# Hybrid encoder trunk on one core: M4 parts of four late pairs kept in freed operand slots, row block 0 of the last block finished first, one page's place in the plan, and one wide attention product

## The chip, the core and the metric

The kernel runs on one NeuronCore of a Trainium2 chip. The metric is device time in microseconds (us). The kernel before has a median of 2621.29 us over three runs (2619.23 to 2624.82).

The engines, as the profile names them: PE multiplies matrices (PEld loads its stationary operand beside it), DVE is the vector engine, ACT the scalar engine, POOL the general one; SP only issues DMAs, POOL issues some too. Each engine takes its instructions strictly in the order in which the program wrote them. An instruction whose input is not there holds everything behind it on that engine.

## What is computed

Two layers over `x` (256 rows of 4096). In each layer one wide input projection, then two kinds of heads, then an output projection added to the input; a last norm at the end.

```python
for l in range(DEPTH):                        # DEPTH = 2
    h = rmsnorm(x, norm_w[l])
    proj = h @ w_in[l]                        # 4096 x 11264
    aq, ak, av, ag, rq, rk, rv, rg = jnp.split(proj, SPLIT_POINTS, axis=-1)
    ...                                       # axial rope, qk-norm
    a_out = silu(ag) * gqa_attention(aq, ak, av)
    r_out = silu(rg) * rmsnorm(bidirectional_retention(rq, rk, rv), ret_norm[l])
    x = x + jnp.concatenate([a_out, r_out], axis=-1) @ w_out[l]   # 4096 x 4096
return rmsnorm(x, final_norm)
```

## The kernel before, in words

**Blocks, pairs and pages.** A projection is cut into blocks of 1024 output columns: 11 for each input projection and 4 for each output projection, 30 in all. The four projections are phases 0 to 3. Within a block the 4096-long contraction is cut into 16 pairs of 256. For a pair, rows (two blocks of 128), contraction (two halves) and columns (two of 512) are the 2x2x2 blocks of a matrix product. A "seven" pair (7 or 8 of the 16) forms it with seven block products M1 to M7 in Strassen's manner; the other, "eight" pairs use eight products that go into the banks M2 to M5. M1 to M7 are seven PSUM banks, which add up over all 16 pairs. A weight page is 128x1024 f32: an eight pair has the pages A and B, a seven pair A, T, B and U, of which T and U are sums (`wsum`) that DVE makes from the two loaded pages.

**Split numbers.** Every f32 operand is split in two fp32r numbers: the high part (`whi`, `fhi`, `whb`) is a cast on ACT, the low part (`wlo`, `wlb`) is source minus high part on DVE. "Far" pages take a road without DVE: ACT casts (`fhi`), ACT writes minus that (`flo`), and a DMA on POOL's queue adds the source to it. The activations are split in the same way and kept in SBUF all phase long (`x7h`/`x7l` for sevens, `x8h`/`x8l` for eights, `xm` for one mixed pair). A product is three matmuls of 128x512: high x high, high x low, low x high.

**The end of a block.** `combining` adds the banks into two result tiles, in the order M1 (copied by ACT), M6, M7, and then M3, M5 (two adds), M4, M2. In PE's stream the last pair (15) is sorted by that same bank order, so that its pages A and B alternate: M3 of A, M3 of B, M5 of A, and so on. The next block starts with M1 and M3 of pair 0, and then needs M3, M5, M4, M2 for page A of pair 1: a bank may be started again only once its add is done.

**What sets the order.** The program plans while it is written: every engine has a clock with a cost per instruction, and each time an engine's clock is the earliest, `pick` chooses what it does next. Weight operations have a key, the planned time of their page (`g.at`) less a lead. Everything else runs in lanes, generators that yield the engine they want next; `Lane.step` works out from when on a lane may go on. `urgent` lanes, `combining` among them, go before weight operations. So a change of a planned time moves instructions in all of the program.

**The last block** (phase 3, block 3) has its own end, `last_combining`. For the last four eight pairs (7, 9, 11, 13) the products into M4 are left out at first and done at the very end from four extra pages, PAGE_E, which are loaded and split a second time. Banks are finished in the order M2, M5, M3, M4, so that the upper 128 rows (row block 0) are complete before M4 is. `finish(m)` then squares, sums, takes the power -0.5 on POOL, scales eight tiles of 128x512 and stores them, all by DMAs on SP's queue.

**Attention values.** `attention_values` multiplies the transposed probabilities with the values, for two heads e, with a product of 256 columns for each.

Of the kernel before, what the change touches and what calls it, by code (L numbers as in the profile page):

```python
# [12 lines left out]
F32R = mybir.dt.float32r  # L13
# [169 lines left out]

def pages_in_order(phase, first=False, last=False):
    late = [_p for _p in range(NP - 1) if _p not in SEVENS[phase]][-LATE_PAIRS:] if last else []
# [7 lines left out]
    for _p, _k in order:  # L193
        if _p in SEVENS[phase] and _p not in skip:
            yield _p, _k, [(_b, (ALL, _a), _h) for _b, _a, _pg, _h in SEVEN_PRODUCTS if _pg == _k]
        else:
# [3 lines left out]
                if _pg == _k and not (_p in late and _b == "M4")  # L200
            ]
    for _p in late:
        yield _p, PAGE_E, [("M4", (_i, 1), _i) for _i in range(2)]
# [3 lines left out]
FINAL_ORDER = ("M2", "M5", "M3", "M4")  # L207
# [115 lines left out]
def hybrid_encoder(  # L323
# [184 lines left out]
    class Weights:  # L508


        def __init__(self):
            self.pages, at = [], 0.0
            for phase in range(2 * DEPTH):
                w = w_out if phase % 2 else w_in
                for b in range(N_OUT2 if phase % 2 else N_IN):
                    start = (phase, b) == (0, 0)
                    end = (phase, b) == (2 * DEPTH - 1, N_OUT2 - 1)
                    for n, (p, k, uses) in enumerate(pages_in_order(phase, start, end)):
# [7 lines left out]
                        at += (MM4 if g.direct else 3 * MM[NB]) * len(uses)  # L526
                        self.pages.append(g)
            self.raws, self.highs, self.sums, self.fars = Slots(RAWS), Slots(HIGHS), Slots(SUMS), Slots(FAR)
            self.lows, self.halves = Slots(LOWS), Slots(HALVES)
            self.todo, self.ops = [], {"V": [], "A": [], "F": []}  # L530
# [35 lines left out]
        def load(self, most=99):  # L566
            while self.todo and most and self.raws.ready():
# [5 lines left out]
                if g.kind == PAGE_E:  # L573
                    step = 1
                for i in range(0, 2, step):
                    n = i if g.kind == PAGE_E else k
                    at = dma("sync", r[:, i : i + step, :], g.src[n, :, i : i + step, :])
# [41 lines left out]
        def high_ready(self, g):  # L619
            s = self.source(g)[0]  # L620
            return s is not None and s[1]() and (self.halves if self.half(g) else self.highs).ready()

        def high(self, g):
# [5 lines left out]
            else:  # L629
                self.highs.take()  # L630
                g.hi = t(wp, [P, 2, NB], "whi", HIGHS, F32R)
            ac.copy(g.hi, f32(src))
# [7 lines left out]
        def low(self, g):  # L640
# [4 lines left out]
            else:  # L645
                self.lows.take()
                g.lo = t(wp, [P, 2, NB], "wlo", LOWS, F32R)
            ve.tensor_sub(g.lo, src, f32(g.hi))
# [10 lines left out]
        def far_ready(self, g):  # L659
            return self.has(g, "raw") and self.fars.ready()  # L660

        def far_parts(self, g):
            self.fars.take()
            src = f32(g.raw[0])
            g.hi = t(wp, [P, 2, NB], "fhi", FAR, F32R)
            g.lo = t(wp, [P, 2, NB], "flo", FAR, F32R)
            ac.copy(g.hi, src)
# [4 lines left out]
        def far_low(self, g):  # L672
            ac.activation(g.lo, f32(g.hi), AF.Copy, scale=-1.0)
            self.adds.append((ac.done, g))

        def add(self):
            while self.adds and self.adds[0][0] <= now.t:
                g = self.adds.pop(0)[1]
                g.low_at = dma("gpsimd", g.lo, g.src[1], accum_op=ALU.add)
# [30 lines left out]
    class Lane:  # L710
# [4 lines left out]
        def __init__(self, steps, need=0, own=0, owner=None, after=0.0, hurry=False, due=1e9, start=lambda: True):  # L715
            self.hurry, self.start, self.due = hurry, start, due
            self.steps, self.need, self.own, self.owner = steps, need, own, owner
            self.begun, self.done, self.want, self.at, self.last = False, False, 0.0, after, after

# [13 lines left out]
        def step(self):  # L733
# [515 lines left out]
    def attention_values(g, h, kv, sgT):  # L1249
# [8 lines left out]
        for e in range(2):  # L1258
            for k in range(MT):
                product(  # L1260
                    o[:, e, :].rearrange("p (k t) -> p k t", t=BLK),
                    at(v, ALL, k),
                    [in_both(w, 2 * e + k) for w in parts],
                    k == 0,
                    k == MT - 1,
                )
# [249 lines left out]
    def block(after_pair, phase, first_order=False, order=LAST_ORDER, last=None):  # L1516
# [9 lines left out]
        for p, k, uses in pages_in_order(phase, first_order, last is not None):  # L1526
            if k == PAGE_E:
                rest_units += [(p, k, use, "H") for use in uses] + [(p, k, use, "L") for use in uses]
                continue
# [16 lines left out]
        for p, k, _, _ in units:  # L1546
            left[p] = left.get(p, 0) + 1
            uses[p, k] = uses.get((p, k), 0) + 1
# [388 lines left out]
```

## Time and profile before

| | us |
|---|---|
| median of three runs | 2621.29 |
| the profiled execution | 2623.02 |
| its span in the profile | 2621.2 |
| PE busy | 2582.6 |
| DVE busy | 2323.9 |
| ACT busy | 1910.0 |
| POOL busy | 436.2 |

The table's busy times can be read against the span: PE has work in nearly all of it, and DVE in nearly nine tenths. A matmul's end is modelled, so that a busy PE need not be one at full rate. Two things are to be kept apart when PE is read: time in which it waits, and time in which its granted clock is below one.

### The profile page before, as it was taken

To read this page: it belongs to the slowest core of one execution; us is meant where nothing else is said; L and a number is where in the kernel's file an instruction comes from. 1 tells how busy PE (TensorE), PEld (TensorE's weight loads), DVE (VectorE), ACT (ScalarE), POOL (GpSimd) and SP (SyncE) were. 2 spreads that over 40 slices of the span, in tenths; PEclk is the share of its full clock that TensorE was granted. 3 is DMA by queue.
4 is the path that set the end of the run, shared out by engine and by line. 5 is a ranking of instruction groups with operands and counts; after the bars stand their busy time and mean duration, and the time that the engine had idled before them with its cause. 6 is when DMAs were issued, how large, how long until landed. Compare 5 with 4: busy or idle time off the path is not lost.

```text
span 2621.2 us, 34650 instructions
## 1 busy us (share of the span) xinstructions
PE 2582.6 (99%) x11570; PEld 2124.0 (81%) x11570; DVE 2323.9 (89%) x2908; ACT 1910.0 (73%) x2672; POOL 436.2 (17%) x592
## 2 busy tenths in 40 slices
PE   9999999999999999999999999999999999999997
PEld 5788888888888888788788888888888888877886
DVE  7898988998888889888998889989989888997888
ACT  8777776777767688666877776767768676886665
POOL 0112211221211110221111211212212121101110
PEclk9999999999999999999999999999999999999999
DMA  9999999998898898999999999989989988989997
GB/s 298 309 296 284 273 285 281 272 300 265 279 281 267 282 272 247 296 281 279 309 270 281 287 277 290 276 267 299 282 263 283 279 263 281 283 243 273 268 275 237
DMA packets 214227, 729.62 MB, mean 278 GB/s; under 512 B 25760, under 2 KB 32544, under 8 KB 214048
## 3 DMA queue, kind: packets, MB, share of 16 engines
q1 hardware_dynamic: 149200, 523.44, 56.7%
q0 software_dynamic: 64848, 203.98, 34.3%
q8 instruction: 90, 1.47, 0.2%
q14 instruction: 89, 0.73, 0.1%
HBM read 679.08 MB, written 48.23 MB: 277 GB/s over the span
## 4 chain that ended last, share of the span: by engine, by line
PE 80%; DVE 7%; issue 4%; DMA 4%; ACT 2%; POOL 1%; SPq 0%; DVEq 0%; ACTq 0%; POOLq 0%
PE M L1111 77%; DVE wlo L232 3%; PE ps L1111 3%; DMA wraw<-in_w_in 1%; DVE wsum L232 1%; DMA pT<-p_dram 1%; ACT whi L232 1%; DMA flo<-in_w_in 1%; DVE cb L232 1%; DMA q<-q_dram 0%; DVE ca L232 0%; ACT fhi L232 0%; DMA q_dram<-cb 0%; DVE x8l L232 0%; DVE wlb L232 0%
## 5 line engine op out<-in xcount | busy, mean ns | idle before, releaser
L232 ACT CAST whi<-wraw 128x1024 fp32r<-128x1024 f32 x525 | 547.0, 1048 | 203.8 <-PE M L1111 172.8
L232 DVE TENSOR_TENSOR wlo<-wraw,whi 128x1024 fp32r<-128x1024 f32 x525 | 636.2, 1220 | 51.7 <-ACT whi L232 24.9
L232 DVE TENSOR_TENSOR wlo<-wsum,whi 128x1024 fp32r<-128x1024 f32 x432 | 526.2, 1218 | 116.7 <-PE M L1111 111.7
L232 ACT CAST whi<-wsum 128x1024 fp32r<-128x1024 f32 x432 | 453.2, 1049 | 142.4 <-PE M L1111 125.8
L1111 PE MATMUL M<-whi,x7h 128*128 128x512 f32 x1248 | 487.8, 391 | 0.0
L1111 PE MATMUL M<-whi,x7l 128*128 128x512 f32 x1248 | 486.2, 390 | 0.0
L1111 PE MATMUL M<-whi,x8h 128*128 128x512 f32 x1060 | 415.7, 392 | 6.2 <-DVE ca L232 3.1
L1111 PE MATMUL M<-whi,x8l 128*128 128x512 f32 x1060 | 414.5, 391 | 0.0
L1111 PE MATMUL M<-wlo,x7h 128*128 128x512 f32 x1248 | 386.4, 390 | 0.7 <-DVE wlo L232 0.7
L1111 PE MATMUL M<-fhi,x8h 128*128 128x512 f32 x844 | 328.8, 390 | 0.0
L1111 PE MATMUL M<-fhi,x8l 128*128 128x512 f32 x844 | 328.8, 390 | 0.0
L232 ACT CAST fhi<-wraw 128x1024 fp32r<-128x1024 f32 x215 | 226.0, 1051 | 136.6 <-PE M L1111 103.0
L1111 PE MATMUL M<-wlo,x8h 128*128 128x512 f32 x1060 | 315.9, 394 | 4.3 <-DVE wlo L232 4.1
L348 POOL DMA_DIRECT2D flo<-in_w_in x157 | 140.9, 897 | 1057.1 <-ACT flo L232 969.0
L232 DVE TENSOR_TENSOR wsum<-wraw 128x1024 f32<-128x1024 f32 x216 | 263.1, 1218 | 14.7 <-DMA wraw<-in_w_in 11.9
L1111 PEld LDWEIGHTS M<-whi,x7h 128*128 128x128 f32 x1248 | 234.9, 188 | 48.5 <-issue 0.5
L1111 PEld LDWEIGHTS M<-whi,x7l 128*128 128x128 f32 x1248 | 234.7, 188 | 48.7 <-issue 0.5
L1111 PEld LDWEIGHTS M<-wlo,x7h 128*128 128x128 f32 x1248 | 233.2, 188 | 49.6 <-DVE wlo L232 2.3
L1111 PEld LDWEIGHTS M<-whi,x8h 128*128 128x128 f32 x1060 | 199.9, 189 | 51.3 <-DVE ca L232 6.6
L1111 PEld LDWEIGHTS M<-wlo,x8h 128*128 128x128 f32 x1060 | 200.3, 190 | 48.5 <-DVE wlo L232 7.8
L232 ACT ACTIVATE flo<-fhi 128x1024 fp32r<-128x1024 f32 x215 | 228.3, 1062 | 6.8
L1111 PEld LDWEIGHTS M<-whi,x8l 128*128 128x128 f32 x1060 | 199.9, 189 | 41.0
(257 smaller groups left out, 3762.5 us busy)
## 6 DMA issues: line engine op xcount, KB each, us to landing
wraw<-in_w_in SPq DMA_DIRECT2D x703, 512.0 KB, 5.9
wraw<-in_w_out SPq DMA_DIRECT2D x256, 512.0 KB, 6.1
flo<-in_w_in POOLq DMA_DIRECT2D x157, 512.0 KB, 8.7
flo<-in_w_out POOLq DMA_DIRECT2D x58, 512.0 KB, 8.5
full<-next_dram POOLq DMA_DIRECT2D x18, 512.0 KB, 8.8
p_dram<-room POOLq DMA_DIRECT2D x64, 128.0 KB, 4.2
pT<-p_dram POOLq DMA_DIRECT2D x16, 512.0 KB, 9.1
next_dram<-room POOLq DMA_DIRECT2D x40, 128.0 KB, 6.2
```

What stands on the lines that cost most here:

```text
L232: return call(out, *args, **kwargs)
L348: getattr(nc, name).dma_start(to, src, **kw)
L1111: nc.tensor.matmul(out, a, b, start=start, stop=stop)
```

## The change

1. *Late pairs.* PAGE_E is gone. For pairs 7, 9, 11 and 13 of the last block the part of page A or B that goes with M4 is written by the split itself, once, to a freed slot: the two pages of pair 7 into operand slots of eights that are done (`x8h`/`x8l`), those of 9, 11 and 13 into slots of sevens (`x7h`/`x7l`). The splits of these eight pages become two instructions of 512 columns each, and their far accumulates two DMAs. The 24 matmuls at the end stay.
2. *Row block 0 early.* The bank order of the last block becomes M2, M3, M5, M4. The adds of rows 0 come first and `finish(0)` becomes a lane of its own; the tile `cb` of row block 1 is completed, squared and multiplied by the norm's gain before M4 is there, so that `finish(1)` has one square and one small operation left ahead of the power. Odd tiles are stored from POOL's queue. The residual rows of the last block are loaded by two DMAs of 512 KB into the `wsum` slots, rather than by four of 256 KB into operand slots, when the last T and U pages are split.
3. *Place of the last pair's page B.* Its planned time moves ahead by nine matmuls in every block, to its first use in the bank order.
4. *Wider product.* `attention_values` does both heads with one product of 512 columns.
5. *Planner.* A lane that wants the engine on which it has just worked no longer waits for that engine's last result to be through; each engine's last end counts by itself. The adds of the residual in the output projections (`out_tasks`) wait, in the plan, until POOL's queue holds nothing else (`calm`).

```diff
+LATE = tuple(_p for _p in range(NP - 1) if _p not in SEVENS[2 * DEPTH - 1])[-LATE_PAIRS:]
...
-FINAL_ORDER = ("M2", "M5", "M3", "M4")
+FINAL_ORDER = ("M2", "M3", "M5", "M4")
...
+                        g.held = (PAGE_A, PAGE_B).index(k) if end and p in LATE else None
+                        if p == NP - 1 and k == PAGE_B:
+                            g.at -= 3 * 3 * MM[NB]
...
+        def pieces(self, g, v, kind):
+            if g.held is None:
+                return v
+            tag = self.tag_of(g)
+            n, blocks = (EIGHT_ALWAYS, 6) if tag == "x8" else (SEVEN_ALWAYS, 7)
+            w = t(ap, [P, blocks, P], tag + kind, n, F32R)[:, :4].rearrange("p k s -> p (k s)")
+            return (w, v[:, 1, :]) if g.held == 0 else (v[:, 0, :], w)
+        def each(self, g, src):
+            if g.held is None:
+                return [(g.hi, g.lo, src)]
+            return [(g.hi[h], g.lo[h], src[:, h, :]) for h in (g.held, 1 - g.held)]
...
-            self.at = self.last
             for e, c in clocks.items():
                 if c.until != before[e]:
+                    self.ends[e] = c.until, c.done
                     self.last = max(self.last, c.done)
-                    self.at = max(self.at, c.until if e == w else c.done)
+            self.at = max([self.after] + [u if e == w else d for e, (u, d) in self.ends.items()])
...
-        for e in range(2):
-            for k in range(MT):
-                product(
-                    o[:, e, :].rearrange("p (k t) -> p k t", t=BLK),
...
+        for k in range(MT):
+            product(
+                o.rearrange("p e (k t) -> p e k t", t=BLK),
+                at(v, ALL, k),
+                [w.rearrange("p (k e i t) -> p i e k t", e=2, i=MT, t=BLK)[:, k] for w in parts],
...
-        urgent.append(Lane((last or combining)(acc, fin, c, order)))
+        (lanes if last else urgent).append(Lane((last or combining)(acc, fin, c, order)))
...
+    def calm(n):
+        moves.run()
+        return not weights.adds and len(moves.queue["gpsimd"]) < n
     def out_tasks(l, n, c):
         for i in range(2):
+            yield lambda: calm(1)
             landed = dma("gpsimd", c[i], residual(l, 2 * n + i), accum_op=ALU.add)
...
+        for b, v in zip(order, (ca, cb, cb)):
+            yield finished(fin, b)
+            yield "V"
+            ve.tensor_add(v[:, 0, :], v[:, 0, :], acc[b])
+        urgent.append(Lane(finish(0, c, None), after=ve.done))
...
+        square(cb[:, 1, :], sums[:, 1, N_OUT - 2 : N_OUT - 1])
+        yield "V"
+        mean_of(ss[:, 0:1], sums[:, 1, : N_OUT - 1])
+        yield "V"
+        ve.tensor_mul(cb[:, 1, :], cb[:, 1, :], fn[1])
+        yield finished(fin, "M4")
+        yield "V"
+        ve.tensor_add(ca[:, 1, :], ca[:, 1, :], acc["M4"])
+        yield from finish(1, c, ss)
...
-            dma("sync", out[m * P : (m + 1) * P, columns(n)], v)
+            queue = nc.gpsimd if n % 2 else nc.sync
+            queue.dma_start(out[m * P : (m + 1) * P, columns(n)], v)
```

How the order moves, at three places on DVE. In these rows M1 to M7 are the banks, `wlo` and `wlb` low parts, `wsum` a sum page.

First place: the end of the first output block of layer 0 (the one of layer 1 is alike), from the add of M6 to the add of M2. Before:

```order
L232 TENSOR_TENSOR cb_9697<-ca_9696,M6_9040 128x512
L232 TENSOR_TENSOR wlo_9746<-wraw_9598,whi_9715 128x1024
L232 TENSOR_TENSOR ca_9696<-cb_9697,M7_8993 128x512
L232 TENSOR_TENSOR wlo_9760<-wraw_9675,whi_9724 128x1024
L232 TENSOR_TENSOR cb_9697<-cb_9697,M3_8946 128x512
L232 TENSOR_TENSOR wlo_9774<-wsum_9692,whi_9735 128x1024
L232 TENSOR_TENSOR cb_9697<-ca_9696,M5_8963 128x512
L232 TENSOR_TENSOR cb_9697<-cb_9697,M5_8963 128x512
L232 TENSOR_TENSOR wsum_9794<-wraw_9711,wraw_9733 128x1024
L232 TENSOR_TENSOR ca_9696<-ca_9696,M4_8971 128x512
L232 TENSOR_TENSOR wlb_9803<-wraw_9622,whb_9742 128x512
L232 TENSOR_TENSOR ca_9696<-ca_9696,M2_8978 128x512
```

The same place now, with the next two rows:

```order
L233 TENSOR_TENSOR cb_9649<-ca_9648,M6_8992 128x512
L233 TENSOR_TENSOR ca_9648<-cb_9649,M7_8945 128x512
L233 TENSOR_TENSOR cb_9649<-cb_9649,M3_8898 128x512
L233 TENSOR_TENSOR cb_9649<-ca_9648,M5_8915 128x512
L233 TENSOR_TENSOR cb_9649<-cb_9649,M5_8915 128x512
L233 TENSOR_TENSOR wlo_9714<-wraw_9550,whi_9667 128x1024
L233 TENSOR_TENSOR ca_9648<-ca_9648,M4_8923 128x512
L233 TENSOR_TENSOR ca_9648<-ca_9648,M2_8930 128x512
L233 TENSOR_TENSOR wlo_9737<-wraw_9627,whi_9676 128x1024
L233 TENSOR_TENSOR wlo_9748<-wsum_9644,whi_9687 128x1024
```

Of the five weight operations that stood between the adds one is left; the others come behind M2.

Second place: the end of the last output block of layer 0, where the last pair's page B has its low part. Before (it is the row with `whi_11941`):

```order
L232 TENSOR_TENSOR wlo_11935<-wraw_11745,whi_11920 128x1024
L232 TENSOR_TENSOR wsum_11946<-wraw_11844,wraw_11878 128x1024
L232 TENSOR_TENSOR wsum_11957<-wraw_11844,wsum_11946 128x512
L232 TENSOR_TENSOR wsum_11957<-wsum_11957,wraw_11878 128x512
L232 TENSOR_TENSOR cb_11932<-ca_11931,M6_11264 128x512
L232 TENSOR_TENSOR wlo_11971<-wraw_11797,whi_11941 128x1024
```

Now (the row with `whi_11867`):

```order
L233 TENSOR_TENSOR wlo_11863<-wraw_11673,whi_11848 128x1024
L233 TENSOR_TENSOR wsum_11873<-wraw_11776,wraw_11797 128x1024
L233 TENSOR_TENSOR wlo_11886<-wraw_11722,whi_11867 128x1024
L233 TENSOR_TENSOR cb_11859<-ca_11858,M6_11214 128x512
L233 TENSOR_TENSOR ca_11858<-cb_11859,M7_11178 128x512
L233 TENSOR_TENSOR wsum_11904<-wraw_11776,wsum_11873 128x512
```

The low part of page B stands three instructions earlier, ahead of the second sum and of M6.

Third place: the end of the program, up to the add of M4 (the last bank). `last` is the factor of a row, `x8h` and `x8l` hold the final norm's gains for the last two column blocks. Before:

```order
L232 TENSOR_TENSOR wlo_23629<-wraw_23516,whi_23609 128x1024
L232 TENSOR_TENSOR cb_23550<-cb_23550,M3_22957 128x512
L232 TENSOR_TENSOR wlo_23641<-wraw_23538,whi_23618 128x1024
L232 TENSOR_REDUCE last_23646<-sums_20734 128x1
L232 TENSOR_SCALAR last_23646<-last_23646 128x1
L232 TENSOR_SCALAR cb_21489<-cb_21489,last_23646 128x512
L232 TENSOR_SCALAR cb_22183<-cb_22183,last_23646 128x512
L232 TENSOR_SCALAR cb_22875<-cb_22875,last_23646 128x512
L232 SCALAR_TENSOR_TENSOR ca_23549<-ca_23549,last_23646,x8h_23229 128x512
L232 SCALAR_TENSOR_TENSOR cb_23550<-cb_23550,last_23646,x8l_23231 128x512
L232 TENSOR_TENSOR ca_23549<-ca_23549,M4_22980 128x512
```

Now:

```order
L233 TENSOR_REDUCE last_23550<-sums_20638 128x1
L233 TENSOR_SCALAR last_23550<-last_23550 128x1
L233 TENSOR_REDUCE rst_23546<-sums_20638 128x1
L233 TENSOR_SCALAR rst_23546<-rst_23546 128x1
L233 TENSOR_SCALAR cb_21393<-cb_21393,last_23550 128x512
L233 TENSOR_SCALAR cb_22087<-cb_22087,last_23550 128x512
L233 TENSOR_SCALAR cb_22779<-cb_22779,last_23550 128x512
L233 SCALAR_TENSOR_TENSOR ca_23467<-ca_23467,last_23550,x8h_23133 128x512
L233 SCALAR_TENSOR_TENSOR cb_23468<-cb_23468,last_23550,x8l_23135 128x512
L233 TENSOR_TENSOR cb_23468<-cb_23468,x8l_23135 128x512
L233 TENSOR_TENSOR ca_23467<-ca_23467,M4_22880 128x512
```

The low parts of weights between the adds are gone. The scaling of row block 0 still stands ahead of the add of M4, with one more operation, the gain on `cb` of row block 1.

More of the change, by code (lines that the diff above doesn't have):

```diff
@@ L1601, in block @@
                 done.append(p)
+                if last and p not in MIXED and p < NP - 1:
+                    weights.holds["x7" if g.seven else "x8"].give(pe.until + PE_PASS)
                 if part == "D":
@@ new lines, in last_combining, with residuals @@
+        yield finished(fin, "M4")
+        yield "V"
+        ve.tensor_add(ca[:, 1, :], ca[:, 1, :], acc["M4"])
+        yield from finish(1, c, ss)
+    def residuals(l):
+        yield lambda: not any(v.kind in (PAGE_A, PAGE_T, PAGE_B, PAGE_U) and v.seven and v.low_at is None for v in weights.pages[-40:])
+        for i in range(2):
+            v = t(wp, [P, 2, NB], "wsum", SUMS)
+            landed = dma("sync", v, residual(l, N_OUT - 2 + i))
+            rest.update({(i, m): v[:, m, :] for m in range(MT)})
+        yield landed
+        rest["at"] = landed
```

148 lines of the change are left out of this document (84 added, 64 removed).

## The prediction

> **What bounds the kernel now.** I read the page's head first, then PE's waits, then busy time by stretches of time, and then the timeline at the places where PE waits longest.
>
> ```profile
> span 2621.2 us, 34650 instructions
> PE 2582.6 (99%) x11570; PEld 2124.0 (81%) x11570; DVE 2323.9 (89%) x2908; ACT 1910.0 (73%) x2672; POOL 436.2 (17%) x592
> PE M L1111 <- DVE wlo L232: 4.8, 3, 3.4
> PE ps L1111 <- DVE pTl L232: 3.2, 6, 0.7
> PE M L1111 <- DVE ca L232: 3.1, 5, 1.0
> ```
>
> PE bounds all but the end. An edit is worth something only where it takes matmul time away, ends a wait of PE, or shortens what follows PE's last matmul. The three lower rows (total us, times, longest) are PE's largest waits in the whole run; all three are for DVE. They look small, but some cost more than the wait, as the stretches show (columns: stretch, length, busy PE, PEld, DVE, ACT, POOL, granted PE clock, DMA share, GB/s):
>
> ```profile
> 77.80:81.20 3.40, 1.55 (x7) 1.03 (x6) 1.24 (x2) 3.34 (x7) 0.00 (x0) 1.00 1.05 393
> 81.30:84.60 3.30, 3.30 (x9) 2.63 (x8) 3.27 (x9) 3.30 (x9) 0.00 (x0) 0.50 0.94 338
> 1060.90:1064.20 3.30, 1.57 (x5) 0.60 (x4) 3.30 (x6) 1.50 (x2) 0.86 (x1) 1.00 0.90 286
> 1064.40:1067.60 3.20, 3.05 (x7) 2.47 (x8) 2.63 (x5) 1.05 (x1) 2.45 (x2) 0.50 0.96 202
> 1306.70:1310.00 3.30, 0.19 (x1) 0.00 (x0) 3.23 (x5) 1.86 (x2) 0.00 (x0) 1.00 0.53 179
> 1310.10:1313.40 3.30, 3.15 (x7) 2.48 (x8) 3.30 (x6) 2.04 (x7) 0.87 (x1) 0.50 0.78 235
> 2358.00:2361.30 3.30, 1.73 (x7) 0.74 (x5) 3.30 (x5) 1.94 (x2) 0.85 (x1) 1.00 0.81 264
> 2361.50:2364.70 3.20, 2.83 (x7) 2.13 (x7) 3.06 (x4) 1.04 (x1) 1.76 (x2) 0.50 0.94 202
> ```
>
> Four times a stretch in which PE idled for about half or more is followed by one at clock 0.50. At half clock 3.3 us do the work of 1.65, so each of the four costs some 1.6 us on top of its wait.
>
> [...]
>
> **End of the first output block, layers 0 and 1 (planner, page B).** This is the first place of the order.
>
> ```profile
> 1061.48 1.22 DVE L232 TENSOR_TENSOR wsum<-wraw 128x1024 f32<-128x1024 f32 x1
> 1061.61 0.51 PE L1111 MATMUL M<-whi,x8h 128*128 128x512 f32 x1 [0.61 <-DVE cb L232]
> 1062.61 0.68 DVE L232 TENSOR_TENSOR ca<-ca,M 128x512 f32<-128x512 f32 x1
> 1063.35 0.50 PE L1111 MATMUL M<-whi,x8h 128*128 128x512 f32 x1 [1.00 <-DVE ca L232]
> 1063.81 0.68 DVE L232 TENSOR_TENSOR ca<-ca,M 128x512 f32<-128x512 f32 x1
> 1064.55 0.79 PE L1111 MATMUL M<-whi,x8h 128*128 128x512 f32 x1 [0.47 <-DVE ca L232]
> ```
>
> PE stands three times, 0.61 + 1.00 + 0.47 = 2.1 us, since the adds that free the banks M5, M4 and M2 stand behind weight operations for pages that PE wants later. In the new order two low parts (a `wlo` is as long as the `wsum` above, 1.22 us), that sum and a `wlb` (as long as an add, 0.68) no longer stand ahead of M2's add: 4.3 us of DVE. That is more than the 2.1 us, so the adds then wait for PE and no longer PE for them. I take 2.1 + 1.6 = 3.7 us here and the same at 2358, where the order and the stretches repeat: 7.4 us. What is put back has to be done afterwards; DVE is busy for only 2.63 of the next 3.20 us and can catch up. Bounds: 0, if PE then waits as long for the low parts, and 7.4. I take the upper end, as the time saved ahead of the adds is twice what is needed.
>
> **End of the last output block, layer 0 (page B).** The second place of the order.
>
> ```profile
> 1305.80 1.22 DVE L232 TENSOR_TENSOR wsum<-wraw 128x1024 f32<-128x1024 f32 x1
> 1307.05 0.69 DVE L232 TENSOR_TENSOR wsum<-wraw,wsum 128x512 f32<-128x512 f32 x1
> 1308.98 1.22 DVE L232 TENSOR_TENSOR wlo<-wraw,whi 128x1024 fp32r<-128x1024 f32 x1
> 1310.25 0.79 PE L1111 MATMUL M<-wlo,x8h 128*128 128x512 f32 x1 [3.36 <-DVE wlo L232]
> ```
>
> This is PE's longest wait: page B's low part starts at 1308.98, behind the second sum and M6's add. Now it follows the first sum directly, so it starts 1308.98 - 1307.05 = 1.9 us earlier and leaves 1.4 us of the 3.36. Whether the clock then still falls is open (1.57 us idle of 3.30 were enough before 2361). I count the 1.9 and two thirds of 1.6: 3.0 us. Around this place two transposes and several splits of operands move too, so the bounds are 0 and 5.0, the whole wait and the clock.
>
> **The start (planner).**
>
> ```profile
> 77.86 0.62 ACT L232 CAST dist<-wide 128x512 bf16<-128x512 f32 x1 [7.62 <-DMA wide<-in_consts]
> 79.98 0.51 PE L1111 MATMUL M<-whi,x8h 128*128 128x512 f32 x1 [1.85 <-ACT whi L232]
> ```
>
> ACT stands 7.62 us before a cast whose load comes late on SP, and the `whi` that PE wants stands behind it. In the new order two small casts between the two go ahead of that wait, about as long as the `dist` row together, 0.6 us. The load's own place on SP, and what it waits for, stay. I take 0.6; bounds 0, and 1.85 + 1.6 = 3.4 if the wait goes.
>
> **The wide product.**
>
> ```profile
> 2144.78 1.43 PE ps L1111 x12
> 2362.09 238.30 PE M L1111 x1044
> ```
>
> In the chain of waits twelve matmuls of 256 columns take 1.43 us, and 1044 of 512 columns 238.30, or 0.228 each, so that six take 1.37. Sixteen calls (two layers, four groups, two pairs of heads) give 16 x 0.06 = 1.0 us. The moving operand is gathered in runs of 32 columns before and after; no row shows a price for that. Bounds 0 and 1.2.
>
> **The end.** The third place of the order.
>
> ```profile
> 2604.00 0.68 DVE L232 TENSOR_TENSOR cb<-cb,M 128x512 f32<-128x512 f32 x1
> 2605.87 0.73 PE L1111 MATMUL M<-wlo,x8h 128*128 128x512 f32 x2
> 2606.76 1.28 DVE L232 TENSOR_SCALAR cb<-cb,last 128x512 f32<-128x512 f32 x3 [0.69 <-POOL last L482]
> 2609.28 0.68 DVE L232 TENSOR_TENSOR ca<-ca,M 128x512 f32<-128x512 f32 x1
> 2610.81 0.60 ACT L232 ACTIVATE M<-cb 128x512 f32<-128x512 f32 x1
> 2611.99 0.55 POOL L482 TENSOR_TENSOR last<-last,half 128x1 f32<-128x1 f32 x1 [5.26 <-DVE last L232]
> 2617.20 0.59 SPq L348 DMA_DIRECT2D out<-cb  x1
> 2608.00:2610.00 2.00, 0.00 (x0) 0.00 (x0) 1.96 (x4) 0.71 (x2) 0.00 (x0) 1.00 0.83 312
> 2618.00:2620.00 2.00, 0.00 (x0) 0.00 (x0) 0.00 (x0) 0.00 (x0) 0.00 (x0) 0.50 0.82 320
> ```
>
> M4 is complete on PE at 2605.87 + 0.73 = 2606.6, but its add starts at 2609.28, behind the scaling of row block 0, which starts at 2606.76 because the last add of row block 0 stood behind low parts until 2604.00. From 2608 to 2620 the DMA engines carry the results at nearly their full share, also after the last issue on SP has ended at 2617.8: twelve us that begin when the first tile is scaled.
>
> On PE row block 0 is complete 30 matmuls ahead of the end, 30 x 0.228 = 6.8 us, at 2599.8. Without low parts in between, one add of it and three of row block 1 follow (4 x 0.6), two reductions (0.3) and the power (0.55): scaling starts near 2603.1, 3.7 us earlier, and takes 2.5 us (2606.76 to 2609.28) and one operation of 0.6 more. So M4's add comes at 2606.2, and it waits for PE. One square (0.8) is gone and the sum is shorter; the second power comes at 2608 instead of 2611.99. The first tile is 3.7 us earlier, the twelve us of transfers as well, and the second row block is ready within them. I take 3.6; the last low parts, for which PE waits some tenths, lie inside this. Bounds: 1.5, if the residual loads land late ahead of DVE's adds or POOL's issues hold up a tile, and 5.
>
> **Edits that cost nothing here.** Without PAGE_E, four loads, four casts and four low parts go; eight pages split in two instructions each, which costs some 0.15 us more a page on ACT and DVE (2 x 0.68 for 1.22), and four more DMAs go on POOL's queue. Their cover: from 2362 until 2600.4 PE runs without a wait, in the chain's row above. Were it gone, that would cost 1 to 2 us. `calm` moves residual adds behind far pages on POOL's queue; POOL is busy for 17%, and the results are wanted tens of us later. The two new loads on SP wait for the last sums, when no other load stands behind them.
>
> **Sum.** 7.4 + 3.0 + 0.6 + 1.0 + 3.6 = 15.6 us. All of the order moves, and which new waits PE gets can't be read from the old trace: I allow 1.5 us, three like the 0.47 above, which leaves 14.1. The profiled execution took 2623.02, its span and 1.8 us around it; so 2608.9 for it. The median of the runs lies 1.7 us lower, and so does my forecast: 2607.
>
> **Rivals.**
> *The waits change places.* The adds are early, and PE stands as long for the low parts behind them, at half clock too. Then the end and the product alone count: 2621.3 - 4.6 = 2617 (2613 to 2619). For it: DVE is busy for 3.30 of 3.30 us before each of these half clocks. Against: 4.3 us move to cure 2.1, and DVE has 0.57 us free right behind.
> *More goes.* At the start, at 1306 and in PE's waits for attention operands everything ends: 2.8 + 2.0 + 3.2 = 8 us more, 2599.
> *Slower.* The combining adds now go ahead of a low part at nearly every block's end.
>
> ```profile
> 443.41 1.22 DVE L232 TENSOR_TENSOR wlo<-wraw,whi 128x1024 fp32r<-128x1024 f32 x1
> 445.85 1.09 PE L1111 MATMUL M<-wlo,x8h 128*128 128x512 f32 x4
> ```
>
> At this one the low part is done at 444.6 and wanted at 445.85: 1.2 us to spare, and one add takes 0.6. If it came 1.8 us later, 29 ends would cost 0.6 us each, 17 us, and half clock after six of them 10 more: 2607 + 27 = 2634. It decides from where the low part comes over 1.2 us later than now; over about 0.5 us lost at each end, the kernel is slower.
> [...]
>
> **Chances.** Forecast, with the last rival in it, 0.55 (own range 2601 to 2613); changed places 0.22; more 0.1; slower 0.13. The range leaves out the slower case and the lower half of "more": 2598 to 2619. A measurement of this kernel tells some 0.2%, 5.2 us, from no change, so faster is below 2616. The forecast, "more" and two fifths of the changed places are faster, 0.74; the rest of the changed places is the same, 0.13; slower 0.13.
>
> **What would show it.** Right: no wait for `ca` or `cb` near 1061 and 2358 and no clock of 0.50 after them; the wait near 1306 under 2 us; M4's add within 1 us of PE's last matmul, and the second power less than 3 us after it; twelve attention matmuls become six. Wrong: PE's waits for `wlo` above 5 us in total, half clocks at new places, the last adds on DVE waiting for the residual's load.

## The result

| | before | after |
|---|---|---|
| median of the runs, us | 2623.04 (2619.23 to 2638.11, 6 runs) | 2605.26 (2602.49 to 2608.61, 6 runs) |
| profiled execution, us | 2623.02, span 2621.2 | 2605.90, span 2604.1 |
| PE's last matmul starts, us from the span's start | 2606.2 | 2591.4 |
| from there to the end of the span, us | 15.0 | 12.7 |

The ratio is 0.9926, 95% interval 0.9901 to 0.9951. The same kernel again, in another set of runs, gave 0.9938 (0.9924 to 0.9952) with a median of 2605.20. One run of the six before, at 2638.11, pulls the first ratio down; by the means of the other times it is 0.9936, an estimate from the times on record, and nearer to the second. The forecast was 2607, so the number holds. Parts of its reasoning do not, as the experiments show.

The page's head and PE's waits in the changed kernel (total us, times, longest):

```profile
span 2604.1 us, 34418 instructions
PE 2573.2 (99%) x11474; PEld 2114.9 (81%) x11474; DVE 2320.9 (89%) x2910; ACT 1910.5 (73%) x2680; POOL 444.8 (17%) x604
PE M L1146 <- DVE wlo L233: 3.4, 6, 0.8
PE M L1146 <- ACT whi L233: 2.1, 2, 1.9
```

There is no row for `ca` or `cb` any more, and the longest wait for a low part is 0.8 us where it was 3.36. The places of the prediction, by stretches of the changed kernel (columns as in the prediction):

```profile
79.38:82.79 3.41, 1.64 (x7) 1.37 (x8) 1.63 (x3) 3.26 (x5) 0.00 (x0) 1.00 0.98 375
82.79:86.20 3.41, 2.98 (x14) 2.14 (x13) 3.38 (x9) 2.45 (x5) 0.00 (x0) 1.00 0.75 254
1061.00:1064.00 3.00, 3.00 (x15) 2.49 (x14) 3.00 (x4) 2.97 (x4) 0.44 (x1) 1.00 0.26 87
1304.50:1308.00 3.50, 3.50 (x17) 2.80 (x15) 3.46 (x7) 0.97 (x1) 0.00 (x0) 1.00 1.02 412
1308.00:1311.00 3.00, 2.33 (x11) 1.72 (x10) 3.00 (x4) 2.97 (x5) 1.42 (x2) 1.00 0.94 356
2345.00:2348.00 3.00, 3.00 (x15) 2.49 (x14) 3.00 (x5) 2.64 (x3) 0.00 (x0) 1.00 0.14 16
```

PE runs through the ends of both first output blocks, and its granted clock stays at 1.00 from 11 us until after PE's last matmul. The stall at the start, though, is still there, and as long as before (row of the timeline):

```profile
81.15 0.50 PE L1146 MATMUL M<-whi,x8h 128*128 128x512 f32 x1 [1.89 <-ACT whi L233]
```

The end, from the changed kernel's timeline (start, length, engine, line, operation, and in brackets the wait before it):

```profile
2588.57 1.28 DVE L233 TENSOR_SCALAR cb<-cb,last 128x512 f32<-128x512 f32 x3 [0.35 <-POOL last L1818]
2591.38 0.39 PE L1146 MATMUL M<-x7l,x8h 128*128 128x512 f32 x1
2591.81 0.69 DVE L233 TENSOR_TENSOR ca<-ca,M 128x512 f32<-128x512 f32 x1
2593.59 0.57 POOL L1818 TENSOR_TENSOR last<-last,half 128x1 f32<-128x1 f32 x1 [1.57 <-DVE last L233]
```

The transfers there, by stretches of the changed kernel:

```profile
2590.00:2592.00 2.00, 1.77 (x8) 1.13 (x6) 1.97 (x4) 0.52 (x1) 1.66 (x4) 1.00 0.85 316
2600.00:2602.00 2.00, 0.00 (x0) 0.00 (x0) 0.00 (x0) 0.00 (x0) 0.00 (x0) 0.50 0.84 312
2602.00:2604.00 2.00, 0.00 (x0) 0.00 (x0) 0.00 (x0) 0.00 (x0) 0.00 (x0) 0.50 0.01 4
```

M4's add starts as PE ends, the second power 1.8 us later. The DMA engines' share is 0.84 to 1.03 from 2590 to 2602, twelve us as in the kernel before (0.82 to 1.02 from 2608 to 2620); they now begin before PE ends and not behind it.

### The profile page after: what moved, and what is told of

Same layout as the page of the kernel before. It is cut to its first block, busy times and chain, and to the rows that moved or that the text cites. A ratio compares the mean times of both kernels' runs of the same rounds, so it can differ in the third digit from the quotient of the medians.

```text
span 2604.1 us, 34418 instructions
## 1 busy us (share of the span) xinstructions
PE 2573.2 (99%) x11474; PEld 2114.9 (81%) x11474; DVE 2320.9 (89%) x2910; ACT 1910.5 (73%) x2680; POOL 444.8 (17%) x604
## 4 chain that ended last, share of the span: by engine, by line
PE 83%; DVE 5%; DMA 5%; issue 3%; ACT 2%; POOL 1%; SPq 0%; DVEq 0%; POOLq 0%; ACTq 0%
PE M L1146 80%; PE ps L1146 3%; DVE wlo L233 2%; DMA wraw<-in_w_in 2%; DVE wsum L233 1%; DMA q<-q_dram 1%; DMA wraw<-in_w_out 1%; ACT whi L233 1%; DMA pT<-p_dram 1%; DMA flo<-in_w_out 0%; DVE cb L233 0%; ACT fhi L233 0%; DMA x<-in_x 0%; DVE ca L233 0%; DMA next_dram<-room 0%
## 5 line engine op out<-in xcount | busy, mean ns | idle before, releaser
L233 ACT CAST whi<-wraw 128x1024 fp32r<-128x1024 f32 (+1 forms) x521 | 540.6, 1045 | 196.5 <-PE M L1146 149.6
L233 DVE TENSOR_TENSOR wlo<-wraw,whi 128x1024 fp32r<-128x1024 f32 (+1 forms) x521 | 628.9, 1215 | 50.1 <-ACT whi L233 30.1
L1146 PE MATMUL M<-whi,x8h 128*128 128x512 f32 x1048 | 408.8, 390 | 2.2 <-ACT whi L233 2.1
L1146 PE MATMUL M<-whi,x8l 128*128 128x512 f32 x1048 | 408.0, 389 | 0.0
L233 ACT CAST fhi<-wraw 128x1024 fp32r<-128x1024 f32 (+1 forms) x215 | 224.3, 1043 | 145.0 <-PE M L1146 91.6
L1146 PE MATMUL M<-wlo,x8h 128*128 128x512 f32 x1048 | 308.6, 390 | 2.0 <-DVE wlo L233 2.0
L233 ACT ACTIVATE flo<-fhi 128x1024 fp32r<-128x1024 f32 (+1 forms) x215 | 226.5, 1054 | 7.5 <-PE M L1146 0.7
```

Source lines behind the costliest of these rows:

```text
L233: return call(out, *args, **kwargs)
L1146: nc.tensor.matmul(out, a, b, start=start, stop=stop)
```

## The experiments

All ratios are to the kernel before, run in the same set. Some parts were put into the kernel before, alone or together (e1 to e5, e11), some taken out of the changed kernel (e6, e7, e9). The new end was not put alone into the kernel before.

**The planner's reckoning alone (e1).**

```diff
-            self.at = self.last
             for e, c in clocks.items():
                 if c.until != before[e]:
+                    self.ends[e] = c.until, c.done
                     self.last = max(self.last, c.done)
-                    self.at = max(self.at, c.until if e == w else c.done)
+            self.at = max([self.after] + [u if e == w else d for e, (u, d) in self.ends.items()])
```

> The kernel before with the planner's new reckoning of a step's time alone. In the order one operation, not five, now stands between the seven combining adds of the first output block of each layer. My theory (the prediction's 3.7 us at each of the two ends): PE's three waits for the banks there (2.1 us each) and the half clock behind them (1.6 us each) are gone, the two other half clocks (near 81 and 1310 us) stay, and the time falls by 7.4 us: ratio 0.9972. Rival A (the waits change places): the 4.2 us of waits come back as waits for low parts, ratio 0.999 to 1.001. Rival B (the half clocks are a matter of where a pause falls on a fixed grid of 3.413 us, on which the four of the kernel before lie, and not of these waits): the waits go, 4.2 us, and the number of half clocks is anything from 0 to 4, 1.7 us each.

Measured: 0.9996 (0.9984 to 1.0008), no change. The bank waits and their half clocks were gone at both ends, as in the theory, but two new stalls ate the gain. The first begins on POOL. Its issues near the end of the first output block, from the timeline of the kernel before:

```profile
1061.82 0.86 POOL L348 DMA_DIRECT2D flo<-in_w_out  x1 [12.32 <-ACT flo L232]
1064.99 1.22 POOL L348 DMA_DIRECT2D ca<-in_x  x1 [2.31 <-DVE ca L232]
1065.71 1.72 POOL L348 DMA_DIRECT2D cb<-in_x  x1
```

And from the timeline of this one, with the matmul on PE that waits for the last of them:

```profile
1058.69 1.23 POOL L348 DMA_DIRECT2D ca<-in_x  x1 [11.69 <-DVE ca L232]
1059.42 1.73 POOL L348 DMA_DIRECT2D cb<-in_x  x1
1060.16 1.91 POOL L348 DMA_DIRECT2D flo<-in_w_out  x1
...
1076.46 0.89 PE L1112 MATMUL M<-flo,x8h 128*128 128x512 f32 x2 [2.26 <-DMA flo<-in_w_out]
```

PE's stretches there in this kernel:

```profile
1073.50:1076.90 3.40, 1.14 (x6) 0.64 (x5) 2.63 (x4) 3.40 (x10) 0.00 (x0) 1.00 1.04 272
1076.90:1080.30 3.40, 3.40 (x10) 2.63 (x9) 1.21 (x1) 2.43 (x3) 3.05 (x6) 0.50 1.03 318
```

The combining adds now end earlier than the far page's copy, so the two residual adds of 512 KB go ahead of the far page's add on POOL's queue. The far page's add issued at 1060.16 landed 16.3 us after its issue, the next one 13.6; in the kernel before, where no residual add stood ahead of the first, the two took 7.0 and 8.5. PE waits 2.26 us, works for a third of the stretch (1.14 of 3.40), and a half clock follows. The second stall, at the end, is shown at e5.

**Page B's earlier place alone (e2).**

```diff
                         g.at, g.high_at, g.low_at = at, None, None
+                        if p == NP - 1 and k == PAGE_B:
+                            g.at -= 3 * 3 * MM[NB]
```

> The kernel before with the earlier place of the last pair's page B alone. My theory: the wait of 3.36 us at the end of layer 0's last output block falls to about 1.4, the time by 3.0 us (ratio 0.9989), and the three bank waits of 2.1 us at the ends of the first output blocks stay, as five operations still stand between the adds there. Rival: the earlier page B was itself needed for the ends of the first output blocks: then the bank waits there go too, and the time falls by 7 to 10 us (0.9965).

Measured: 1.0023 (1.0014 to 1.0033), slower. The longest wait near 1306 did fall, to 1.4 us, but the adds of other blocks came later: PE's waits for `ca` rose from 3.1 us in five to 8.3 in eleven (row of PE's waits below), and a half clock follows three new ones for `cb` and `ca` near 1320 (2.7 us). In this profile PE's last matmul is 6.0 us later than in the kernel before, and 3.8 of these are there by 340 us, so the adds are not the whole of it.

```profile
PE M L1113 <- DVE ca L232: 8.3, 11, 1.0
```

**The wide product alone (e3).**

```diff
-        for e in range(2):
-            for k in range(MT):
-                product(
-                    o[:, e, :].rearrange("p (k t) -> p k t", t=BLK),
...
+        for k in range(MT):
+            product(
+                o.rearrange("p e (k t) -> p e k t", t=BLK),
```

> The kernel before with the wide attention product alone (96 matmuls of 512 columns in place of 192 of 256). My theory: 1.0 us less, ratio 0.9996, and the four stalls of the kernel before with their four half clocks stand where they stood, since the order of the other work is nearly the same. Rival A: the gather in runs of 32 columns is dearer over 512 columns, each of the 96 takes over 0.24 us, no gain or up to 2 us lost. Rival B (grid): the stalls stand but the half clocks behind them are fewer or elsewhere, and the time falls by 1.0 us and 1.7 us for each that is missing.

Measured: 1.0001 (0.9993 to 1.001). PE's last matmul starts at 2605.2 and not 2606.2. That this is the 1.0 us expected is chance, as waits and half clocks differ between the two profiles; the runs can't tell it from nothing. What the product itself gives shows where no wait falls into it. First attention's twelve narrow matmuls, from the chain of waits of the kernel before; then, from that of the changed kernel, two products that lie near each other:

```profile
347.26 1.45 PE ps L1111 x12
...
2120.85 1.43 PE ps L1146 x12
2137.27 1.42 PE ps L1146 x6
```

The last two are, in the changed kernel's groups of that stretch by form, retention's product as before (`vh`, `wTh`) and attention's in its new form (`pTh`, `kv`):

```profile
L1146 PE MATMUL ps<-pTh,kv 128*128 128x512 f32 x4 | 1.4, 400 | 0.0
L1146 PE MATMUL ps<-vh,wTh 128*128 128x256 f32 x4 | 1.1, 282 | 0.0
```

So attention's product takes 1.42 us where it took 1.45: 0.03 us a call, 0.5 us for the sixteen. A wide matmul takes 0.237 us here, where the other ones of 512 columns take 0.228; the 0.009 between them may be the price of the gather, which no run separates. The third half clock was near 1296 here, not 1310.

**These three together (e4).**

> The kernel before with these three together: the planner's reckoning, page B earlier, the wide product; the end of the program, the pages of M4 and the residual's loads are those of the kernel before. My theory: 7.4 + 3.0 + 1.0 and some tenths at the start, 11.4 to 12 us, ratio 0.9955; what the whole change gains beyond it, about 4 us, is its new end. Rival: the parts undo each other (an order that suits one shifts the others' pages): 4 to 8 us, ratio 0.997 to 0.9985, and the new end is worth more than the 3.6 us that I gave it.

Measured: 1.0012 (1.0001 to 1.0023). Neither theory; the three parts together are a little slower than none. The stall for `flo` is there again, larger (timeline), and so is the one at the end. PE also waits 2.62 us for a `whi` near 2574, with a half clock behind it. The stall for `flo`:

```profile
1082.12 1.19 PE L1114 MATMUL M<-flo,x8h 128*128 128x512 f32 x4 [2.98 <-DMA flo<-in_w_out]
```

**The three and calm (e5).**

```diff
+    def calm(n):
+        moves.run()
+        return not weights.adds and len(moves.queue["gpsimd"]) < n
+
     def out_tasks(l, n, c):
         for i in range(2):
+            yield lambda: calm(1)
             landed = dma("gpsimd", c[i], residual(l, 2 * n + i), accum_op=ALU.add)
```

> The three parts of the run before together with calm (residual adds issued only once POOL's queue is empty); what is still missing of the whole change is its end: pages of M4 held in operand slots, the order of the last blocks, the scaling and the result's queues. Theory of interplay: without calm PE waited 2.98 us for one far page (flo) near 1082 with a half clock behind it, 3.0 + 1.7; calm takes these 4.7 us away, and the time is 2625.3 - 4.7 = 2620.6 (ratio 0.9995); all the rest of the gain, some 15 us, is the new end's. The prediction's theory, calm costs and gains nothing: 2625 (1.0012). Rival: the three parts cost in many small places that neither calm nor the end touches, 2625 again, but with the wait for flo gone and others in its place.

Measured: 0.9958 (0.9946 to 0.9969), a median of 2611.66: calm is worth 13.6 us on top of the three, three times what the theory gave it. What is left to the changed kernel lies in the last 20 us, where the old end now stops PE twice (timeline of e5):

```profile
2587.26 1.22 DVE L232 TENSOR_TENSOR wlo<-wraw,whi 128x1024 fp32r<-128x1024 f32 x1
2588.53 0.74 PE L1114 MATMUL M<-wlo,x8h 128*128 128x512 f32 x2 [1.50 <-DVE wlo L232]
2589.70 1.28 DVE L232 TENSOR_SCALAR cb<-cb,last 128x512 f32<-128x512 f32 x3 [0.69 <-POOL last L482]
2592.22 3.49 DVE L232 TENSOR_TENSOR wlo<-wraw,whi 128x1024 fp32r<-128x1024 f32 x3
2593.50 0.74 PE L1114 MATMUL M<-wlo,x8h 128*128 128x512 f32 x2 [3.29 <-DVE wlo L232]
```

With the new reckoning the old end's adds and the scaling of row block 0 go ahead of the last low parts. The new end needs no low parts there: M4's pages are split earlier and held.

To see where each part acts I compared when the same matmul, by its number, starts in each profile, against e3, which has as many matmuls. In us, below zero is earlier; the head is e3's time:

```
                  60   340  1047  1098  1280  1333  2356  2406  2587  last
three (e4)      -0.3   2.4   3.5   3.9   4.0   1.3   1.5  -1.5   3.0  10.3
with calm (e5)   1.8   3.1   4.4  -0.1  -0.9  -7.5  -9.0 -13.2 -13.2  -7.2
changed          2.0   4.4   3.4  -1.2  -1.9  -7.9  -9.5 -13.2 -13.0 -13.8
changed again   -0.1  -2.4  -2.3  -6.9  -7.6 -12.8 -12.2 -16.5 -16.3 -17.1
```

Calm turns +0.4 into -4.5 between 1047 and 1098, and -2.7 into -6.6 between 1280 and 1333. Between 2406 and 2587 it is +4.5 and 0, since the wait near 2574 is gone; I did not trace by what. On top of these four the new end is worth 6.6 us, all of it in the last 20 us.

**The changed kernel without calm (e6).** The line `yield lambda: calm(1)` is out.

> The changed kernel without calm alone. Theory of interplay: the wait for flo near 1080 comes back, 3.0 + 1.7 us: ratio to the kernel before 0.9926 + 0.0018 = 0.994. The prediction's theory: calm is nothing, 0.9926. Rival: with the residual adds ahead of far pages at all the ends of output blocks, several waits for flo of 1 to 3 us come, 0.996 or more.

Measured: 0.9978 (0.9966 to 0.999), some 10 us lost against the repeated 0.9938, more than the first two theories gave; but there is one large wait for `flo`, not several. PE waited 3.0 us for `flo` near 1077, with a half clock, as in e4. From 1047 to 1098 it lost 5.0 us against the changed kernel, from 1280 to 1333 3.1; that is 8 of the 11.4 us that lie between the two profiles at PE's last matmul.

What calm does on POOL's queue shows in the changed kernel's timeline:

```profile
1063.56 1.23 POOL L349 DMA_DIRECT2D ca<-in_x  x1 [11.70 <-DVE ca L233]
1064.30 1.41 POOL L349 DMA_DIRECT2D flo<-in_w_out  x1
1084.69 1.58 POOL L349 DMA_DIRECT2D cb<-in_x  x1
```

The first residual add still goes ahead of the far page's; only the second is held back, by some 20 us. The far page's add landed after 7.0 us with no residual add ahead of it (kernel before), 13.0 with one (changed kernel) and 16.3 to 17.0 with two (e1, e4, e6). With 13.0 PE doesn't wait for it.

**The changed kernel with the old reckoning (e7).** The edit of e1, taken back.

> The changed kernel with the planner's reckoning of before. The prediction's theory: three bank waits at the end of each first output block (2.1 us) with a half clock where the grid falls on them (1.7 us each) come back, 4.2 to 7.6 us: ratio to the kernel before 0.9942 to 0.9955. Rival: without the new reckoning other waits go (it had three new ones of 2 to 2.6 us in the first run), so that it is as fast as the changed kernel, 0.992 to 0.993.

Measured: 0.9983 (0.9974 to 0.9992), some 12 us lost against 0.9938, more than the 4.2 to 7.6 expected. From PE's waits:

```profile
PE M L1145 <- DVE ca L233: 7.8, 11, 1.0
```

The three bank waits, 2.1 us, are back at both first output blocks (no half clock behind them this time), and, as in e2, at the ends of the blocks after them.

**The clock by itself (e8).** A kernel that leaves out the whole computation; groups of matmuls with pauses made of VectorE's operations:

```
        ps = pm.tile([P, NB], F32, tag="ps", name="ps", bufs=2)
        for i in range(count):
            nc.tensor.matmul(ps, a, b, start=i == 0, stop=i == count - 1)
        b = wp.tile([P, NB], F32R, tag="b", name="b", bufs=2)
        nc.vector.scalar_tensor_tensor(c[:, :NB], ps, 0.0, raw, op0=ALU.mult, op1=ALU.add)
        nc.vector.tensor_add(c[:, :n], c[:, :n], z[:, :n])
        nc.vector.tensor_add(b, z[:, :NB], c[:, :NB])
```

> A kernel of its own that leaves out the whole computation (it writes zeros): TensorE does 46 to 51 matmuls of 128x128 by 128x512 in a row (some 10.5 to 11.6 us), then pauses while VectorE does one to three operations, 0.8 to some 3.8 us by ten steps, six times over; then runs of 14 groups of 2 to 6 matmuls with a pause of some 0.8 us behind each group, three times over. It asks what makes the clock 0.50. Grid theory: the half clock comes in stretches that are whole multiples of 3.413 us and start on one grid through the whole run; it follows a grid stretch in which PE was busy for less than some share, by the kernels so far between 42% and 48% (1.44 of 3.41 us busy: half clock; 1.64: none); so pauses under 1.7 us never bring it, pauses over 3.7 us always, and those between by their place on the grid; groups of 2 and 3 matmuls (36 and 45% busy) bring it, of 5 and 6 (58 and 63%) don't. Rival A: only a grid stretch without any work brings it: then no pause under 3.4 us does, and no group. Rival B: it is not a grid but the length of the pause since the last matmul, with one threshold near 2 us.

Measured: all changes of clock in the run lie on one grid of 3.413 us. Two stretches of that grid in the view by stretches, each with the next one:

```profile
134.28:137.70 3.42, 1.50 (x6) 1.24 (x7) 1.83 (x2) 0.00 (x0) 0.00 (x0) 1.00 0.02 5
137.70:141.11 3.41, 3.41 (x9) 2.65 (x8) 0.00 (x0) 0.00 (x0) 0.00 (x0) 0.50 0.00 0
707.72:711.13 3.41, 1.59 (x8) 0.97 (x6) 1.75 (x2) 0.00 (x0) 0.00 (x0) 1.00 0.00 0
711.13:714.54 3.41, 2.32 (x10) 1.92 (x11) 1.00 (x2) 0.00 (x0) 0.00 (x0) 1.00 0.00 0
```

I counted each matmul as the 0.227 us from one start to the next (the view's busy time, with modelled ends, reads a little more). Then all 38 full-clock stretches that a half clock follows were busy for at most 41%, and of the 309 that none follows all but 11 for more. No length of a pause decides: one gap of 2.23 us from start to start brought it, and one of 4.09 didn't. So rival A and rival B fall. Some bounds of the grid theory were off too: that gap of 4.09 is a pause of some 3.9 us, over its 3.7; groups of 5 brought the half clock in all three rounds, after a grid stretch of 40.8% in the first, and groups of 3 did not in the third, with 39.9% in six stretches. So in this run the half clock goes with the work of the one stretch, and not with the average of a group and its pause. At half clock, the clock stayed so after stretches of this run that were busy for up to 77%, and was full again after those from 81%.

**Without page B's earlier place (e9).** The edit of e2, taken back.

> The changed kernel without page B's earlier place. The prediction's theory: the low part at the end of layer 0's last output block is late again, 3.0 us: ratio to the kernel before 0.9926 + 0.0011 = 0.9937. Rival A: page B's place is a cost (alone it made the kernel of before 6 us slower, most of it in the first 340 us and at the ends of the second output blocks): then this kernel is faster than the changed one, 0.990 to 0.992. Rival B: with the new reckoning and calm, page B's place no longer matters, 0.9926 within 0.1%.

Measured: 0.995 (0.9937 to 0.9962), a median of 2606.53. The interval overlaps that of the changed kernel run again, whose median is 1.3 us lower. Near 1297 a wait of 2.8 us for `wlo` came, with a half clock, but PE's last matmul still starts 1.1 us earlier than in the changed kernel's first profile. From 1280 to 1333 this profile gains 3.2 us against e3, where the changed kernel gains 6.0 and 5.2 in its two: there page B's place is worth 2 to 3 us. Whether any of that is left in the whole time stays open; it is under what these runs tell.

**The start repaired (e10).**

```diff
-        ac.copy(dist, wide)
-        drop()
...
+            if n == 2:
+                yield lambda: came(4.0)
+                yield "A"
+                ac.copy(dist, wide)
+                drop()
```

> The changed kernel with one repair: the cast of dist goes into ScalarE's queue only when its load has landed by the planner's reckoning, not before. In the changed kernel ScalarE stands 8.45 us for that load near 79 and PE 1.89 us for the cast behind it. Theory: 1.9 us less, ratio to the kernel before 0.9926 - 0.0007 = 0.9919, with the PE stall near 79 gone. Rival A: the cast behind it (whi) waits for its own page, which is late as well, and nothing is gained, 0.9926. Rival B: every step behind is moved by the planner and the sum of PE's waits changes by chance, 2 to 4 us either way.

Measured: 0.9942 (0.9929 to 0.9956), a median of 2605.03, the same as the changed kernel. The stall near 79 is gone, and another has come. From PE's waits of e10:

```profile
PE M L1145 <- DMA flo<-in_w_in: 3.1, 2, 2.5
```

And its stretches:

```profile
120.00:130.00 10.00, 10.00 (x46) 8.28 (x45) 9.27 (x17) 8.11 (x12) 2.35 (x3) 1.00 1.06 289
130.00:140.00 10.00, 7.92 (x35) 6.21 (x34) 9.76 (x26) 7.53 (x22) 1.60 (x2) 1.00 1.10 312
```

PE is 2.9 us earlier at 114, and 0.8 later at 160: it waits 2.5 us for a far page near 138, with the DMA share at 1.06 and 1.10 in these rows. That the load of `x` moved by the repair is the cause is argued, not shown.

**Calm alone (e11).**

> The kernel before with calm alone. In its order the residual adds stand behind the far page's add near 1062 anyhow, and PE waits for no flo there. Theory of interplay: calm undoes a harm that only the new reckoning does, so alone it gives little, 0 to 2 us (ratio 0.9992 to 1.000), with the bank waits near 1061 and 2358 as they were. Rival: calm is worth the same 14 us in any order, ratio 0.995. The prediction's theory: nothing, 1.000.

Measured: 0.9982 (0.9973 to 0.999), between the theories. The bank waits near 1061 and 2358 stay. Between 1271 and 1323 PE gains 4.4 us: the wait near 1306 falls from 3.36 to 1.5, without a half clock. DVE works without a gap up to that low part in both profiles; in the 9.6 us ahead of it, operand splits for the next layer (`x8l`, `x7l`, `xf`, `full`) take some 2.4 us in the kernel before and 1.4 here, which may be part of the 1.9 us; the rest I did not trace. So calm does on its own much of what the prediction gave to page B.

**The changed kernel again (e12).**

> The changed kernel once more, unedited, beside the kernel before: it says how firm the yardstick is for the runs that leave one part out. If the first ratio of 0.9926 holds within 0.1%, the kernel without page B's place (0.995) has lost some 5 us and the one with the repaired start (0.9942) some 4; if it comes out near 0.9945, both are the same as the changed kernel. In the profile: PE's waits for ca and cb near 1061 and 2350 absent again, the stall near 79 there again, 1.9 us, with or without a half clock behind it as the grid falls; of the other waits, those that come again at the same place are the order's, the others the transfers'.

Measured: 0.9938 (0.9924 to 0.9952). Both kernels of e9 and e10 are the same as the changed one within the intervals. No row for `cb` came, and one of 0.4 us for `ca`. PE's wait near 79 was 0.8 us this time. By 340 us this execution was 6.8 us ahead of the first, and by the end 3.3.

## Why the prediction came out

**First output blocks, 7.4 us: right, on a condition that I had priced at nothing.** The adds stand back to back, PE doesn't wait, and no half clock follows. In the table, first profile: 4.6 us between 1047 and 1098, 3.7 between 2356 and 2406, 8.3 in all. But e1 shows that with the new reckoning alone the first of these is given back, since earlier adds release the residual adds earlier, ahead of a far page.

**"Edits that cost nothing here": the step that failed.** The prediction weighed calm by when the results are wanted ("tens of us later") and by POOL's busy share (17%), not by what stands behind the residual adds on POOL's queue. It was worth 4.7 us on its own (e11), 13.6 on top of the three (e4 to e5), some 10 in the whole (e6). Without it the whole change has a median of 2617.45 (e6), which is the 2617 of the rival *the waits change places*. So it is in part luck that the number came out: it holds because a step that was priced at nothing stood in the package.

**Last output block of layer 0, 3.0 us: half of what came, and half of the cause.** From 1280 to 1333 the change gained 6.0 us against e3, 5.2 in the second profile, over the upper bound of 5.0. Without page B's place it gains 3.2 there (e9), without calm 2.9 (e6), so that each is worth 2 to 3 us. Page B alone loses there by new waits for banks (e2); calm alone gains 4.4 (e11). What calm takes out of DVE's way shows only in part (e11).

**The start, 0.6 us: nothing came of it.** PE's stall is 1.89 us where it was 1.85. In the second profile it is 0.8, with the same order. No half clock follows the 1.89 us: the stall now falls across a boundary of the grid, and at 0.227 us a matmul the grid stretch from 79.38 was busy for 44%, the one from 77.86 in the kernel before, which a half clock follows, for 37%.

**The wide product, 1.0 us: over-sized.** It gives 0.5 us by PE's records. The row of 1.43 us at 2144.78 is retention's product; attention's twelve took 1.45, and six wide ones take 1.42 and not 1.37 (e3).

**The end, 3.6 us: nearly right, and worth more beside the new reckoning.** The 84th matmul from the last starts 34.7 us ahead of the span's end in the kernel before, 31.5 in the changed kernel and 31.2 in e7, the new end with the old reckoning: 3.2 to 3.5 us gained. In the changed kernel 2.3 of these lie behind PE's last matmul (12.7 and not 15.0 us), the other 0.9 in PE's last 84 matmuls. What the prediction did not see is that with the new reckoning the old end costs PE 6.6 us more than the new one (e5). That is no gain over the kernel before, where PE ran on without those waits.

**New waits, 1.5 us: not told apart.** By 340 us the first profile was 4.4 us behind e3, the second 2.4 ahead, with the same order. So one execution differs from the next there by more than most terms of the sum.

**The rivals.** Changed places is what e1 and e4 did: without calm and the new end the gains came back as other waits. The slower case did not come; the low parts that now follow the adds cost PE 3.4 us in all. The half clocks went with the waits: neither profile of the changed kernel has one while PE works, and in e8 one followed grid stretches with up to 41% of work.

## What to carry to other kernels

Work that is finished earlier releases what depends on it earlier, and that may go ahead of something urgent in a queue (in e1 the far page's add landed 16.3 us after its issue, in the kernel before 7.0): before an edit that makes a step early, look at what the step issues, on which queue, and what is behind it there. Price a package of edits as a package: here three parts together made the kernel slower, a fourth that looked idle turned them into a gain, and of those run alone none gave more than 0.2%. Where the order of everything moves, compare when the same matmul starts in both profiles; it shows place by place what totals of waits hide.

## What the hardware showed beyond expectation

The granted clock changes on a grid of 3.413 us in these profiles: in the kernel before the four half clocks while PE works are 3.413 us long each, and 75.093 us between two changes are 22 times that. In the profiles of the two kernels and of the eleven runs beside e8, from 15 us to PE's last matmul, the clock fell after 25 grid stretches, PE busy for at most 39.7% of each, and after none of some 9,780 others, busy for 39.9% or more. In e8 the two overlap, between 38 and 41%. So where a stall lay on the grid made a difference: behind the one of 1.85 us near 80 in the kernel before came 3.413 us at half clock, which by their length cost some 1.7 us more (an estimate), behind the one of 1.89 us near 81 in the changed kernel none. The kernel before had four half clocks while PE worked, the changed one none in two executions.
